# The sum of a norm's two halves moves from GpSimd to VectorE, with all queue orders written anew

## The chip, the cores and the metric

One core of one Trainium2 chip runs the whole program in a single launch. The core has five engines, each with its own queue of instructions: TensorE (PE in the profile; its weight loads are PEld), VectorE (DVE), ScalarE (ACT), GpSimd (POOL) and SyncE (SP), which here only issues DMAs. The metric is the device time in microseconds (us). Before the change the median of three runs is 1772.27 us (1771.36 to 1775.65).

## The reference

Two layers over 512 latent tokens and 256 context tokens of width 1024, in float32. Layer 0 has neighbourhood attention beside spatial gating, layer 1 has two-directional retention; each is followed by a gated MLP ("ffn") with a depthwise convolution of width 3. What the change touches is the RMS norm, which stands before and after each of these four parts:

```python
def rmsnorm(x, g):
    xf = x.astype(jnp.float32)
    y = xf * lax.rsqrt(jnp.mean(xf * xf, axis=-1, keepdims=True) + EPS)
    return (y * g.astype(jnp.float32)).astype(x.dtype)
...
        x = x + g1 * rmsnorm(y_lat, norm_g[i, 1])
        h = modulate(rmsnorm(x, norm_g[i, 2]), sh2, sc2)
        x = x + g2 * rmsnorm(conv_ffn(h, ...), norm_g[i, 3])
```

Context tokens go through layer 0 in the same way; only the 512 latent rows are returned.

## The kernel before

Tokens are cut into six tiles of 128 rows (0 to 3 latent, 4 and 5 context). A matrix product in float32 accuracy is made of three float32r products, from a high and a low part of each factor (`split`: L233 on ACT makes the high part, L234 on VectorE the low part; `mm3`: L277 to L280 on TensorE).

The program is a row of long stages (spatial gating and attention to about 330 us, ffn 0 to about 870, retention to about 1395, ffn 1 to about 1750), in which TensorE works through large products. Between two stages lies a **seam**: the output rows of one part must be normed, gated, added to the residual stream, normed again, modulated and transposed before the next part's products can begin. There are three such seams inside the program, one norm at the start (`first_x`) and one at the end, where rows only go out to memory.

For each row tile a seam runs this chain (names as in the profile):

1. L768, VectorE: `y` half = product in PSUM + partial result, two halves of 128x512.
2. L493, ACT: `Square` of each half, with its sum over the row accumulated into one column of `ss` (128x2).
3. `rms`: L498, a `tensor_scalar` on one column: first half's sum + second half's sum + eps. Then `rsq`, L479, GpSimd: that to the power -0.5.
4. L524, VectorE: `y` times the gate, half by half (needed before step 5, not before step 3).
5. L531, VectorE: residual = `y` * r + residual, half by half.
6. L493, L498, L479 again, on the residual (tiles with an x in the name: `wxc`, `xc2r`; those of step 2 and 3 have a y).
7. L543 (VectorE) and L544 (ACT) scale the two halves; then PE transposes (`ht`), and ACT and VectorE apply the modulation (L586, L588, L650, L652) and split the result.

`rms` is called 42 times: 6 at the start, 12 in the seam after attention (`wyb`, `wxb`), 12 after ffn 0 (`wyc`, `wxc`), 8 after retention (`wyd`, `wxd`), 4 at the end (`wye`). The power has no other home than GpSimd in this kernel.

The order of instructions in each engine's queue isn't the order in which the Python code makes them. `queue()` reads a compressed string, `ORDER`, that holds a permutation for each of the five queues, and chains the instructions of each engine in that order. So a waiting instruction holds up everything behind it on its engine. GpSimd's queue also holds DMA issues, among them the sums of retention's weights made by accumulating DMAs in memory (`weight_sums`, L380, tiles `tv` and `tq`), which can lie anywhere before retention uses them.

Of the kernel before, what the change touches and what calls it, by code (L numbers as in the profile page):

```python
# [56 lines left out]
g~h51h5T}T{+3ItR9jj`yQ*t0(Q17IEkLhrt!?FabCW7D0I5j4IrPdZTBoksRl?<af?MbzagN7VN?Z8M>>OpX5Q(jg^0`u~pwg99Oe4K{uDX6Fjw{z^@>
IXNLbM}~xoxEuYNQFvzM^d%(tw)p7WattQ)4wf^xNV^QA#~~_U_qB8#UE69qrA>H*8H$PucgW=!deLrD15MN^hko1t=eeN%{jdE=s|=2Kw!><5~+gI^|v
QussI+9&gZcx!HnkJHBeyY)C#6y_i1JXB!pmJytZ~5Px|@oX0T|Eq;S!iq>b4+wOvB|0(_+4q-$$-*oeV(9O4r`nlPrMrvv1f7`6#kzpbXnp&r<R@(eX9
YoE9V{04E)i?AUA!_M4(bCgRY|{`d#7K0x7uGtogo%uejx8(>duVxhga(I-gW%teR8{_n$MgxwiovU{mK`sdXrt-&I|YU@Ni(-@p+Y`1gFAJZzHyqGY^K  # L60
Y%ULKFmHa2xtWBzq<qWK=`tgNc7D_4&nsOqEcjkcO<bawK@$=<cP+B$0ai1@iU(?Z+le=g`0v`8aAfe$?<j#C5QxAPt1Ct~?g9R33SLlrkH_7A{D>imHl
=5p0@v&U1jw@@vW9Q&W*zY1!Zrn%H&^P#5%-IO|N>0cEui9^|2o)oj65q?tR;}f3{xb=zm3eq5_EuRv16ea(F{DgQz93(n;fG1qBeFx<WbnXqYOtzljP;
8krIb{@uWKwNrj;b@%M4pilu_DL$JbMaW%h38fwc4NGF6a*Nh*%ipFXyha&piknxfg%$74H#@QMBjp#rhS9;x7gLLgc?9{#C5M2Zw(VbF*`^J8*bT{H`G
1ABeZhw@Ln^ZFD1jMXbW`j?>jwCquy{+E!ILdG2Ac?|Jcn{EnEJZloO*(>HHklY^6u=e7|=Z@3Y1dZ(=J^Isg^*gZC?!c0Q9%ZFq&W<6hb5vE{~V{x#Nu
0LNi0ipwt(G5fwsdr?9cJ;z95-g&9`{~-(!XggSGi1DZ#sDNxs+vl?wIyWZ(KbFiPJ=~vAbO`bOn`Ps@d0tan1f1ZrtcJYh|{N7K#vQ5;N9X;F-Qw=?%K
MdoOiz}=<h}AYl8k&?7JfV8EAdx<oWT>qdRxkCxpA#T6|G_MCjx6d2x-9O79Td^D30~b@4U8&-21NF>VWJ`0VCYnKK66a_N>!0|Wg79}x6mL5B{rgLeiw
A`Q@)vu8Tk<L7!`5+4-<{o4U6bi-4^q35`H6MY=_IB}A0y$qr4S7a}Ia)_?Gs;lw}qK(}|YdhZ((XV_;xfm|k2O1eq+U(P@c+MHm!9Yjg=Pe<2<`|$mN7
<4$8#AInjy2UlQL6or_?Z|S`WNwI!Qh%t;@qbN)XqP~9)nnu9~YP#ZpCh1;3oKMxn?K~ydE!YU><bg?3o>eI86pCd?VSnc~yPGTe^pT(x@A#-DiV3#c^N
2Dw#!GEP|fJ(xUPxAdXG4WU>lCSKdP_t7dtMwr!=E@(PFu&8rv>Rc|%GTBYV>BH7x;5C<b_u`-@Ic3-EFvoW?JM5)Vr;<5cF%9?$r-zQp{ZLz5d57qcdH
>u7RkK0>XX8$Y3MW7-FocS&DGd6g8fOB3?qa9EHwc!wER}Xy_Up?ytF&6SHsm3tHcv5K&v862!!IPni92H&?4ZH3Y_X*k#!R#WkImk9ljyl>q+WkCfIEU  # L70
GJkLc%dx3&eXt;a1~K`a&E%+Y&A!M<H=e0*Yx?iUjiM30M)izMReGQ2MIBSBvi)crkCcSZL6K-?v(4h`HRD?ced1qktdPtbP-4E-qgv8S(>I(`Nsf)MZv
# [2281 lines left out]
```

## Time and profile before

| | |
|---|---|
| median of three runs | 1772.27 us |
| the profiled execution, own time | 1771.19 us |
| its span (first to last instruction) | 1769.4 us |
| TensorE busy | 1731.5 us (98%) |
| VectorE busy | 1434.4 us (81%) |
| ScalarE busy | 1122.4 us (63%) |
| GpSimd busy | 448.2 us (25%) |
| L498, the sum, 42 times on GpSimd | 32.09 us |
| L479, the power, in the same stretches | 25.56 us |

Busy time is the union of an engine's instructions. A number in square brackets in a timeline is the time that the engine sat idle before that instruction, and behind the arrow stands what ended the idling. A matmul's end is modelled, so a busy TensorE isn't necessarily one at its peak. A table by windows gives, for each stretch, its length, then the busy time of PE, PEld, DVE, ACT and POOL (instructions in brackets), then the granted TensorE clock, the share of time in which the DMA engines were busy, and GB/s.

### The profile page before, as it was taken

The page shows a single profiled execution, that of the slowest core. Times are in us where ns is not written, and L with a number is a line of the kernel's source. Part 1 is how long each engine was busy: PE and PEld are TensorE (multiplying, and loading weights), DVE is VectorE, ACT ScalarE, POOL GpSimd, SP SyncE. Part 2 cuts the span into 40 slices and gives each one's busy share as a digit, 9 for nine tenths or more (in the row PEclk, how much of TensorE's full clock was granted, in tenths as well). Part 3 has the DMA queues.
Part 4 walks back from the last instruction along what each step waited for, and adds up shares of the span by engine and source line. Part 5 has one row for each costly group of instructions (what it writes and reads, how often), then busy time and mean ns, then how long its engine had stood idle before and what let it go on. Part 6 is the DMA issues. An engine that isn't in the chain of part 4 may idle for free.

```text
span 1769.4 us, 29634 instructions
## 1 busy us (share of the span) xinstructions
PE 1731.5 (98%) x11108; PEld 1563.9 (88%) x11108; DVE 1434.4 (81%) x2408; ACT 1122.4 (63%) x2046; POOL 448.2 (25%) x570
## 2 busy tenths in 40 slices
...
GB/s 299 153 163 177 162 200 107 192 217 240 223 205 231 222 246 229 270 230 250 316 206 71 175 172 155 148 133 163 120 151 144 174 103 169 194 219 186 177 159 125
DMA packets 121292, 330.59 MB, mean 187 GB/s; under 512 B 14222, under 2 KB 36238, under 8 KB 120476
## 3 DMA queue, kind: packets, MB, share of 16 engines
...
## 4 chain that ended last, share of the span: by engine, by line
PE 81%; DVE 7%; ACT 4%; DMA 3%; POOL 3%; issue 2%; DVEq 0%; ACTq 0%; SPq 0%; POOLq 0%
PE px L277 10%; PE wf L278 4%; PE wf L279 4%; PE wf L280 4%; PE xv L277 4%; PE py L277 4%; PE px L280 1%; PE px L278 1%; PE px L279 1%; PE yv L277 1%; PE py L278 1%; PE py L280 1%; PE py L279 1%; PE ug L278 1%; PE wr L278 1%
## 5 line engine op out<-in xcount | busy, mean ns | idle before, releaser
L416 DVE SCALAR_TENSOR_TENSOR acc<-ar,cs,acc 128x512 f32<-128x512 f32 x256 | 188.0, 754 | 9.8 <-DMA acc<-in_adab_row 7.4
L2039 POOL DMA_DIRECT2D yf<-yp x64 | 55.7, 940 | 258.4 <-ACT yp L2035 226.6
L2035 ACT COPY yp<-wf 128x512 f32<-128x512 f32 x118 | 68.6, 584 | 70.5 <-PE wf L280 68.6
L277 PE MATMUL px<-hs,wc 128*128 128x384 f32 (+1 forms) x480 | 112.0, 309 | 0.8 <-ACT pre L1879 0.8
L277 PE MATMUL px<-blk,wb 128*128 128x384 f32 (+1 forms) x480 | 109.0, 308 | 0.0
L1892 DVE SCALAR_TENSOR_TENSOR cv<-pre,cw,cv 128x769 f32<-128x769 f32 (+1 forms) x88 | 77.6, 884 | 27.8 <-ACT cv L1891 27.5
L1891 ACT ACTIVATE cv<-pre,cw 128x770 f32<-128x770 f32 (+1 forms) x88 | 81.3, 926 | 19.3 <-DVE pre L1884 14.0
L277 PEld LDWEIGHTS px<-hs,wc 128*128 128x128 f32 x480 | 82.5, 188 | 6.7 <-ACT pre L1879 1.9
L277 PEld LDWEIGHTS px<-blk,wb 128*128 128x128 f32 x480 | 81.8, 188 | 4.7 <-ACT pre L1879 0.4
L1879 ACT ACTIVATE pre<-px 128x256 f32<-128x256 f32 (+2 forms) x160 | 54.3, 368 | 43.7 <-PE px L277 30.5
L2039 POOL DMA_DIRECT2D yd<-yp x48 | 47.4, 1020 | 124.7 <-ACT yp L2035 122.1
L1895 DVE SCALAR_TENSOR_TENSOR cv<-pre,cw,cv 128x769 f32<-128x769 f32 (+1 forms) x88 | 77.4, 884 | 1.3
L277 PE MATMUL px<-hs,wd 128*128 128x384 f32 x240 | 72.0, 338 | 0.0
L277 PE MATMUL py<-blk,wc 128*128 128x384 f32 x240 | 69.6, 337 | 0.0
L2039 POOL DMA_DIRECT2D yd<-ypg x48 | 45.7, 1006 | 86.5 <-ACT ypg L2035 73.4
L233 ACT ACTIVATE wb<-s 128x512 fp32r<-128x512 f32 x80 | 48.6, 627 | 22.1 <-PE px L277 19.1
L233 ACT ACTIVATE wc<-q 128x512 fp32r<-128x512 f32 x80 | 49.0, 629 | 17.6 <-PE px L277 6.9
L234 DVE TENSOR_TENSOR wb<-s,wb 128x512 fp32r<-128x512 f32 x80 | 54.6, 688 | 4.7 <-ACT wb L233 4.3
L234 DVE TENSOR_TENSOR wc<-q,wc 128x512 fp32r<-128x512 f32 x80 | 54.6, 688 | 4.3 <-ACT wc L233 4.0
L278 PE MATMUL wf<-fo,g 128*128 128x512 f32 x144 | 54.6, 397 | 1.2 <-ACT g L233 1.2
L280 PE MATMUL wf<-fo,g 128*128 128x512 f32 x144 | 55.5, 395 | 0.0
L279 PE MATMUL wf<-fo,g 128*128 128x512 f32 x144 | 55.2, 395 | 0.0
...
## 6 DMA issues: line engine op xcount, KB each, us to landing
...
```

The costliest lines, as they stand in the source:

```text
L233: self.S.activation(hi, src, AF.Copy)
L234: self.V.tensor_tensor(out=lo, in0=src, in1=hi.bitcast(F32), op=ALU.subtract)
L277: mm = lambda *p, **k: self.T.matmul(*p, skip_group_check=True, **k)
L278: mm(out, lhs[0], rhs[0], start=first, stop=False)
L279: mm(out, lhs[0], rhs[1], start=False, stop=False)
L280: mm(out, lhs[1], rhs[0], start=False, stop=last)
L416: V.scalar_tensor_tensor(out=acc[s], in0=raw[:, kk * 512 : kk * 512 + 512], scalar=self.cs[:, 8 * s + k : 8 * s + k + 1], in1=acc[s], op0= ...
L1891: S.activation(d, s, AF.Identity, scale=w1, bias=b)
L1892: V.scalar_tensor_tensor(out=d[:, 1:W], in0=s[:, 0 : W - 1], scalar=w0, in1=d[:, 1:W], op0=ALU.mult, op1=ALU.add)
L1895: V.scalar_tensor_tensor(out=d[:, 0 : W - 1], in0=s[:, 1:W], scalar=w2, in1=d[:, 0 : W - 1], op0=ALU.mult, op1=ALU.add)
L2035: S.copy(v, ps)
L2039: G.dma_start((yd[t] if first else y[t])[:, o], v, accum_op=ALU.add)
```

## The change

In `rms` the sum is issued to VectorE in place of GpSimd:

```diff
     def rms(self, name):
         ss = self.sst.pop(name)
         w = self.bp.tile([P, 1], F32, name=f"w{name}", tag="rsw", bufs=4)
-        self.G.tensor_scalar(out=w, in0=ss[:, 0:1], scalar1=ss[:, 1:2], scalar2=EPS, op0=ALU.add, op1=ALU.add)
+        self.V.tensor_scalar(out=w, in0=ss[:, 0:1], scalar1=ss[:, 1:2], scalar2=EPS, op0=ALU.add, op1=ALU.add)
         return self.rsq(w, name)
```

The similar sum of `rstd` (L484, six times in the spatial gating) and that of retention's own norm (L1661) stay on GpSimd. The rest of the diff replaces the whole `ORDER` string (it also grows by three lines), of which only this is readable:

```diff
 ORDER = """
-c-oD82e>3xb>_LZLRY8i?&_TTb-$c*&N<JE6W+XelXKRLq#0?XQ2?QcB!r|<0wj`z1j3jo8zF&=iN@I8{V+Dci@{)w*WNYjyx#v*zmW!P?{1G?b$4~$Tl
...
 """
```

Decoded as `queue()` does it, the two strings compare so. The instructions are the same but for the 42 sums. Those that keep their order among themselves aside, 4525 of TensorE's 10964 instructions stand elsewhere, 756 of VectorE's 2344, 547 of ScalarE's 1910, 136 of GpSimd's 524 and 104 of SyncE's 484; no instruction is moved by more than 102 places. Some places:

- **Start.** SyncE's first loads were `ar000` (weights of the modulation), `cc`, `xn04`, `xn05` (the first two row tiles); they become `xn04`, `cc`, `xn05`, `ident`, `ar000`. TensorE began with the four products of `ar000` and then had 8 transposes of rows; it now begins with a transpose, and the products of `ar000` stand between the transposes. VectorE's queue becomes sum, scaling (L515), sum, scaling, row by row.
- **After ffn 0.** VectorE's queue around the last rows (2 and 3), before and after:

```
before: L768 yf3 | L588 L588 L234 h1c  L524 yf3  L234 h1c  L524 yf3 | L531 L531 yc3r | L234 rwk
after:  L768 yf3 | L588 L524 yf3  L498 wxc2  L234 h1c  L588  L498 wyc3  L524 yf3  L234 h1c | L531 L531 yc3r | L234 rwk
```

- **After retention.** For row 0, VectorE's order becomes L768, L768, L524, sum `wyd0`, L524, L768 (row 1), L531, L531, L768 (row 1), L524 (row 1), sum `wxd0`, L524 (row 1), sum `wyd1`, L543.
- **After attention.** On GpSimd three DMA issues of the weight sums (`tq23`, `tq13`, `tv13`) move from behind the seam to between its powers of rows 0 to 2.
- **End.** VectorE's last instructions, before: L768 (row 3), L531 (row 2), L524, L524, L531, L531. After: the same, with the sum `wye3` between the second L524 and the first L531. TensorE's last 60 instructions are unchanged.

More of the change, by code (lines that the diff above doesn't have):

```diff
@@ L57 @@
[L57 to L71, printed above, removed]
@@ new lines @@
+l=*yma3U=X~e;&b@E!4$^HzlDr<mE1JQF8}9%<b^fKPHkHUp-V8oGUQ+CQUioZ_Q-sKcA3EMuwfx(gZ!)*|?Qv>;%6E<Vj?#(5bY(b{r^=1H1TF6)dP?A
+ghlPG<1>a-QmInkbS={leFlfh4C(%pdGr}y#pm)T=Nje>(CCYzNd;-@!D<X-5F9{m#dPd|bjvVImx@z{*_6a(+eDw%*muP$YB+cxcnp}4^+$BCKvR@L^Q
+gfH6qQ)kw&ynxaiq5U^56p$ap%04oc2Y034-QS<EtUqtOKHl{(e2rzD7P)uTh-ixT9D6AR4j0_rRJmrrBg(?iZp&vw0&rhMpWwT^5qL?ByA&_n#5l!O%#
+g{S5XpYWe2m_Og4ini8?8Z&f^j$DhK*$Xg|%+WMy%ND8uJWRAPUQGWo*PO++`J+d-M_=ZNMjx79bGmDM%XHG_1TPM#``Cg)G0DpS0R>dqt+$<>t@P1Pp&
+j<mQ?$fNGNcG?|vtq!|`2T$V9+DNTuHL7hrfU?Y?%w*S^PiHd~TJNb`1r>%zDtJf-J>GZ~6{(7bN6@Y!g~G&R?$oHhp`NN~V{Zf1Zqi=btZ$&*O?9<Yi+
@@ new lines @@
+4jb-W(mJhWbOTZLMv$)Zg4jyZ7wI_U68(CLV#>x=!lhDpwQ1yhx$uaI%@Al^(Ch*&2oY1p}4jiaRwnFt^LBHnAm+4Ey}PBf4>r!dz_}!C(*@so6OEqLy~
+6Vp^cv++o(XT#DB;Rv#O>`5g?<(}JEC4%C3JLD!NU8?+3oykX*a9lFKuv)?HW(gZaT!Om&K)!agj)Y43CturCC68n0(sgJseHfW!9i2CIShOTL3xE|Mx<
+M3c@9XbrV#_4=4&R4_BxDkCc>7~9&INVIX4l|fCZ#-C}AEM3lx`YK0j|TaD<`L?mcHh+PqJw5y+pe`uHMd;7jYd&}`MLSIJH-bC4V^qS{<>(mLzGtN@H>
+KUvqT3EmFRBaqr?4OokJ=&<U#SK{CoJ*--#~>Dpk?T;%-4zFN;@1k?7L&%#Xy6#rdmnw3%t#wKIBkbrdb}(?jBU@dDnnJDM7MU8QH`i-Ov&{daM$IT^k>
+)zTbUIvrX1HSwZYjlU^=F25rzlCqgU5cJn#WO!tlK7{)f>8AfFy1yX)f$#YNG4+P{Th!dFJzc)Fr<KQh&lkl{<WJ?J^3Xx_-M&q;@fW@$R?#DuF7k#4wZ
@@ new lines @@
+ZFN@eyG!_l;|I2Q1V@aIH3K;g$y|q*I1&ycQQ0KO{aZ%5S29{v(G0K%=KlK7_6N#Es&(cRW|=`n5-d+x1aFn{S(kUJxr2bcfvi34jU==T7;$nEh=WIX6o
+ml%E1(Ve8+B#-@Aa8{*b?@7cMMUqnT_zb3vfYVQ!Wb=N*Gu3e|Aiwi#%Ulm^y|12oIObuISe^l5VolSK85%HFMLcAnCDjpJ_5^Rc}5%h|fRc-TgFxMCy@
+DlxvxI&jMURua^4Gp$eQl4(RO1FzU1iw+%<xA8%vX}PsqM@-x?AU*R-v64L#|JFV{_Y+-9GMc;lr?Iz+>1o3ymuQ7^6y7b=mX*iV*oJjesQ0eq3rRgNgl
+Y<H{C7n5>E(^_fhef7^FEMM{QkIiLcvuOVHnoR&?So#r`M7KZ@3?+rA~voWdbz*XzRB>zjW?ye!mh^mXxGw^6=q63eu3w-`N5D}mm=?XVVa-Px^E_E%q^
+ZJl?BS8+$`?Msf9POnf!S74S)8#qOSb^EFI9r-v4?d_v;H&6NjAAWSkX9Rk!VEWZvY=U*Q<pTRtwAnv^zYc8d-C*3>^DjD$?TeOX-s>;C69k0e;p=n&fa
@@ new lines @@
+>t0wg4LikYhkbu-V9%k4|Gu9(ecCfVmIfV+>0{8m#<|_^zOe7saoMv6P+O6weBd23Z{aEqG=8HSuXdhK@oJILL%xYI$Ex5=km89dfzNyX6<?=C$=RXCqO
+r;@;>0{cEp4NCV#Y;a4$WbC+QeB}wyOC|ny3F;bY3y;$jTPty*X9ziVZ2bhI+1*kL>Dh*Mf<ny;5*na>xoKiGYv0^!vrK4j_y?w>@oV(DB5@KAqqne{jY
+b9K_(3<o6Tud`=rmGl-N_Q)DkXCAIMO^UtOW90~UG>6x>QoM@O~A_-B{5LSwsBhn;BIipUWRs#VI@Qc9z#A2F^2%pJSfdT=;)DaW@~a4xr&PM3cAM7bca
+aQ&b%zxg73%1%VOXCA~#(#b4v{^)m4${Lv-yS`I=ayn#;LeJ0B4bixg!?$I3CiHy3BD{~`RB=o{iK6EGeS$Bss#=(bR}y8zIDw~UUl(>yGeeu{hik@!Di
+p#OXLRUC>$AA{BAhwl{ql@xzM{6Nf1|5$tu<)prc4e$5FYXT$x>*6o4t3-PeJ}M2Qchg2=FwjD4RD)&~scGLjm6366eR^i6@wnLB_j_dz(v5w~25Ac$L|
@@ new lines @@
++jb%S*ezDA?a$6?^7WTaoQ!;<F-zSQzScR_XZ`{rsJRv<h&Yo%4>J^OZ)kKGa-A=Y|4QXd6^r#mZ=exaF~Eq^U6;qew@42PI#Wzl#W}vh9LmG*)fyqkN&
+(!6>T2DP*xmA~4}ZDi+~9lTB)Fat#D;Qr|U6v?I{D^kL!iJM8sJfxV#Fws6`{jng#H;)RL#_tHGud%jRtTLGhQX|61`wN`C$(AKtoT3@3*p=NTymMDnP@
+vN;gqcB-b_i}_fm%C|uo|2CPo9I#Th?v|lyIBNQw#TU>baA~S)H-|#fNDMeh{(XN9uTKV4~5})MvzkJCD^~3)!WB(4^`wq8B*iLt^TVWuMffLyHb%B({X
+b8;R~=jL?tGRq)*T22Ef(j-Ubu^b4Hb`dnn<pCSXM47<C4NC4g+2+B>|}vKC|@p7zspI-=+xOXP6E7dr->nlq=Shn?|sXBW*;Ql-ky<s~H^i;wJ%gT%Vj
+Fe5^+sHKBNe-PEG?E+PJSZqxB;Tmt?n?8lMPr!(5YI?2DQ9ITM?sIa(jXPeu?)A9bF~c3hfToz#lC;#XuIvC<)$HqN2OnpY%onI;sY|Z`tuDFSt4zFX0+
+)vcw0E4lnLDJhsj<?j<(c4d_lL+1j{}JJq+*mG$pU}389KAWew-Zkx6|qh{)o{wUznx3f@?5rYKkZoJG(lsk5YTtk4*<xTdKkB6pq#me91nJD>@JXphsm
@@ new lines @@
+k2Uv>5^TFW}AZged!)R4d2N)$~i6c_tmRqaceW_^V-2Gy(vN#g6Mm%7)tvSAOfyQ0niZuk>#qf5J4hz9%31%<@lx_qBQ5EA1tg3k+AGI`dLwzw=xC;a=Q
+s;}*9X~;Ics)Y>v?mr{TW@Wi0TMT-Vf}UFgqu-gO?9|~TEpoTcUuq~6J}fv5P2`SCGOY#te~T0Y}_M~CwA)`9ki-a5Bj<s1)`DE?~Bdvic}glzuQ5pyAO
+X$>^?k%UVB~aIp#?{4D)VboACL)o>#>;!0VcKkgi218@gwo6-KCez(r|h6OReCdf#g0)m5Xe)2MSLlEsCMWU&XTXn4ex*TJ(_n_X`3rf_d1AqwD?P8Ad$
+ph-ZFx;lHixN`Z5!|n;SnCt<>IT0pD9y~m2GP78GWqhZ97lmYquS&OP)kriJ-?=LiAXnY+uARH;qv3kU6L4XB0xGnS-Nu)iWDV}gJ&xY*3eh3#7!B8#$J
+tNyC@mU+CS|IksUefigQL3KZwUGgvD8P;V7MEb;uYQV-Ie!<4+<j=k4Ci5jQL1MnJza7x^7f@hiei`w_UxEh>cvmZE&c<UPYaqv}5+xTjo8UsZK_i{Crt
@@ new lines @@
+2gj|&f*pQkqFAVVB4+|>p-N-ub5!W5XbXgP!5OF#@fgq16Yi5rZ#_0p!c5O#|ETpwjTGTvVh^WD#+Pc~CZT^PAMSE+IlC}zTSh}Bb`Jfrm`!j7Zw<{DjD
+AO@f!>S8CTG{HRa79N+2Tt}<ot`4k5Y^_GfVkZ08%hpgIustR8(tr-WY)JF01N5fct#A+fR~I|ycIx9iqC)i!y=&8ww+mLR6Bm+_%3c{b2~n_rwkn-%<%
+bnB$Az7N+2;_VjBptY_U61+~eTZAus}}2!|lSOr3Oa3WKj$4G-D$Net2I$~>h{_9eS1oMw4ePX%%}#(QZyZ5#KG`gYaFVFn2Io)KSSKlN1|yqja!wRF@G
+2TfR^A<dUg1uKh2yok}QsfMwz@}%K#oKXfnU8+h?H$a5zAU}x);0;FT6XIS`YIEHsrly+5Xt=UF80bUfE_Bwo-C*|ji~3wUbumrxRJ6H=M-pC-uO&qbZE
+EfEQiod4|ALcK5e42plW{cHfEaM|Sgl6CBsR0^MbHO|*S4vqQe8Wnrw$iG{?TJc_kb$-3O;;>71&SpE{eHoT2s{LibkqcYKzk_hOgANZJg5<&J<0IFuNK
@@ new lines @@
+!4h$LcD6ldY^TK#_U$39)dO<7OJE~z(p1RtxQJ1@^pUn%mN~Lvr3qop^HUSN(pmS~Ao;x>R)(DyE84O)KmM?&aqz#`97CZ0zD0rn04&Gi_%-V|CGxJqY&
+BXw<p9a=XcLh;0`_kx`Zo~*y;dUV$R`f;u#6AR$T2~wEUX7Vz+^U=#ucI?(`v+k2?tGZ*#A+-xy1cZk8^vz#SfrZ8`Fe@%4F$8pL=RSjBNS>E^I4O5pO}
+k8t8_kGQ_XrD&^<IbRIF4}6zIsn@t+4_`lL8l-@rjNQdb+lUv$rzFu?uoI^Erj@Ch%A#rsws6BjRa_m;e-adL*~YDFNc6$tj(PK%MwvUc`RS0_yOUeWbU
+leE1ks&2a}5rTwgjEVw=Pf_c81lh!0#-A}Wh`_#{6i<oT;~x~jsLzO}#kCWR5<{{45L_>GANm;XT6A^5lkz?LPt9#yJZ0!`2~ef{!~v~T#WsvR@Z5^537
+hqBHtMg@b6oM>8b5rSs&jCdR3Mnm_^4y9DNA{qucf&q0dor^j`eHs#%N?7X1tb5CZ_`+627XoiS5k+4icH3Ika&x)O~YrUoSYaGZU_@<11+w#zbkWX9B~
@@ new lines @@
+*3;_}y-+Scb7+3ekYXAYd<Tx~3-eS$-cDesX{80QvJS2h3_sQ>yx5eGEg1#@*?~3HbOMfYxhiH@jjj%r@UlbeAO;evT3G_>XwqdJ~U)!htH}PM^Z;Lm@*
+Tqg+|EBo4cn12WSowYN=Yk0y9e+wZDNapa;S3Vg<#yUf2ll7U+{tbr;wA#+U?RCTun8#|i;s;)Os!1+Tl@o$OQU%faT)ZqXg*9ImLHNQj-Plz9OV&x245
+$h6GuNT;FNcW=S+_LxMZOmr4z@|Id_`*2X<ljfsYRmv7qHQeNeCq(AE~I51FbQ+x7>yPT@2bf-2j{qk^6gkC$0E=ShfIag=kK{KoFjn@s<U;&lOr|0O|R
+7G~)B6OsE3@fA_dR{R*he#3kdeM$Vf_#g5ez7!lS{RX!&&7Ad1fPmM~kIx9=HZgQCC1Q`TJCbHL(qyX*oVI#Kd`(dJ9s$~ArU#iVkeT&(P>fDIxTU<!Zs
+6R(j9fsQ8@G+MUA)xJ2GVnWKH#mPi$jD@xHFw$QQ4^s)Yh?~QMhK1MjAaM!=Rtz+r~{jJ#dh-5@0$-u1GqC!A&L_5A3IPHPL#5-?3wMjvw7)fVvFA<%a3
@@ new lines @@
+D6&UBvrmD%QN<P}%xr!KjW|cCI?&YO6NAD_Nw6(2uD9rR3qCC=?Sfpmy1-KXu0<Mc!E>lf10VAKHiH426rbw*X1eEQ_m#)}u-x{OUd?Ru1wH?65MvuNwx
+trx0C-dmY;ZoJ7IrWl1b&~nWjlQ{E9FggiRoT0-_fN%2#g#wC&I<gz%rRnhrG(M?FOY5JH|5Kt2(C-J_C71$6nh=^=j5Z3*1s<3WAbUqc1TajC*@0G@bH
+nFPTxevD}vZm=+YZJ5?>e3$W1!@1u=2h`JDWWe5tI?nQh*9eVi?NVPg9-5pLAK-QG`AcAEc}S|2q1%-O9AnMO|;prAWuZ{&E;>als)?zow~HgjeCaZlMS
+*y72)tkB#JvQ8>9-96sjdv@<YAa8}gbWwK?s1cI~cHIe@nx^vY2Zw0XEP!tW-wOtAR40uc>uVh*3Ne#wQ8_&dMA}q$GV{ip)iaB}6h(SC88tZMQ*A*q6?
+Ukif%fg<+Og6!b9P<a4h7@W(PL9@g7?<3)Hr^{Ro~6kKXsB$*HZt3tmE$!L%VjuDeBM@$BqtF(cz(sUB`|Bq{lCtsl69O+cN^2bo!>oJ46=4a{4Cp$87m
@@ new lines @@
+l{QiaffuIjzh%bWHFg&dPg*cL>-;$q}bR9zdD#&b#apW2K4f&RQPQEB@&&k|@yTm8tOP0If`-h*Fw~LPpavUQd0IK>Ly!qm#C*@P}RdF1s0et_2u+vNO8
+L3?&I)CBICJq5GMt~eQ@1tjN<k_-05GQU4O7GL+{e!;Z<^J!1ii1#v+QZ+>^c~_|zdQ48Dy?h>OPt~1!J6kdM+kb@{WQcQO`F-%vaOIAy>HxOW_r7_ura
+;es!Zt1!>WCGiN*Q)T6m0)E-WsD`_OZ+huL@=?#MeYO;GJ6x&@=Yoi1J)Z6+MBtFt^ku(tv6f~N)m6$hZkdWa);&%VulRL-)|aFV4Nlr?<v@R4?nEyMu-
+z+Kfib?4v$wJe}Hyzks)pWU^SI8(Mvb*~A!02AzPJ&Q1T@)RBC*`&Sbi{tkSl9A|W?}^&FqsM?12M-Ov3Z4*6`wr5`FxciPoc_3|tGzV&Fd`OBR6i}~WH
+~jy_{SU^IL8GNw{O#N^goL~69>!*i8sZ8JH!UP1ru2NfnWfCQ_x=l6{zwD;#=~!BozH)lCJgB-288fhb6?f#Ha!oXk+hl7}>9iy^KMd`*<Sb03H9Vd>h5
```

200 lines of the change are left out of this document (81 added, 119 removed).

## The prediction

> **What bounds the kernel now.** I read the page's head first, then a table of the five places where norms run, one window for each, and in the same windows the sums alone.
>
> ```profile
> span 1769.4 us, 29634 instructions
> PE 1731.5 (98%) x11108; PEld 1563.9 (88%) x11108; DVE 1434.4 (81%) x2408; ACT 1122.4 (63%) x2046; POOL 448.2 (25%) x570
> ...
> 0.00:30.00 30.00, 20.81 (x93) 9.72 (x94) 6.54 (x16) 18.16 (x46) 8.11 (x21) 0.89 0.79 283
> 330.00:390.00 60.00, 58.91 (x320) 51.04 (x317) 53.50 (x90) 44.07 (x101) 22.05 (x31) 1.00 0.68 213
> 870.00:912.00 42.00, 37.70 (x214) 31.58 (x213) 37.92 (x62) 31.28 (x75) 20.85 (x28) 1.00 0.93 291
> 1394.00:1428.00 34.00, 29.51 (x172) 25.25 (x172) 30.60 (x56) 24.76 (x60) 11.11 (x16) 0.95 0.50 175
> 1745.00:1770.00 25.00, 16.47 (x72) 13.10 (x70) 16.13 (x25) 6.05 (x17) 7.15 (x9) 0.92 0.33 105
> sum 191.00, PE 163.39 PEld 130.69 DVE 144.69 ACT 124.32 POOL 69.27; mean PE 32.68 PEld 26.14 DVE 28.94 ACT 24.86 POOL 13.85
> ```
>
> TensorE is the bound: it idles 1769.4 - 1731.5 = 37.9 us in all. The windows hold 191.0 - 163.4 = 27.6 us of it: 9.2 at the start, 1.1 after attention, 4.3 after ffn 0, 4.5 after retention, 8.5 at the end. The long stages hold the other 10.3. The change doesn't touch the work of TensorE, so these gaps are all that it can shrink, and within the seams VectorE, at 53.5 of 60 and 37.9 of 42 us, is nearly as full as TensorE.
>
> The next table has the same windows for L498 alone; the last fence is the sum line of the same table for L479.
>
> ```profile
> 0.00:30.00 30.00, 3.42 (x6) 0.89 0.79 283
> 330.00:390.00 60.00, 9.06 (x12) 1.00 0.68 213
> 870.00:912.00 42.00, 10.39 (x12) 1.00 0.93 291
> 1394.00:1428.00 34.00, 6.08 (x8) 0.95 0.50 175
> 1745.00:1770.00 25.00, 3.13 (x4) 0.92 0.33 105
> sum 191.00, POOL 32.09; mean POOL 6.42
> ```
>
> ```profile
> sum 191.00, POOL 25.56; mean POOL 5.11
> ```
>
> A sum of one column takes 32.09 / 42 = 0.76 us on the average. Why so long shows in the timelines of VectorE and of GpSimd at the last rows after ffn 0, with TensorE's largest wait there:
>
> ```profile
> 899.82 0.98 DVE L588 TENSOR_SCALAR hc<-htc,ab 128x256 f32<-128x256 f32 x2
> 900.72 0.68 DVE L234 TENSOR_TENSOR h1c<-hc,h0c 128x512 fp32r<-128x512 f32 x1
> 901.32 0.68 DVE L524 TENSOR_TENSOR yf<-yf,fin 128x512 f32<-128x512 f32 x1
> 901.92 0.68 DVE L234 TENSOR_TENSOR h1c<-hc,h0c 128x512 fp32r<-128x512 f32 x1
> 902.53 0.68 DVE L524 TENSOR_TENSOR yf<-yf,fin 128x512 f32<-128x512 f32 x1
> 904.55 1.41 DVE L531 SCALAR_TENSOR_TENSOR fin<-yf,yc3r,fin 128x512 f32<-128x512 f32 x2 [1.35 <-POOL yc3r L479]
> ```
>
> ```profile
> 900.21 0.30 POOL L498 TENSOR_SCALAR wxc<-ssxc 128x1 f32<-128x1 f32 x1 [2.96 <-ACT jxc L493]
> 900.82 2.54 POOL L498 TENSOR_SCALAR wyc<-ssyc 128x1 f32<-128x1 f32 x1 [0.31 <-DVE hc L588]
> 903.45 0.56 POOL L479 TENSOR_TENSOR xc2r<-wxc,mhalf 128x1 f32<-128x1 f32 x1
> 903.97 0.55 POOL L479 TENSOR_TENSOR yc3r<-wyc,mhalf 128x1 f32<-128x1 f32 x1
> ```
>
> ```profile
> PE rkc L280 <- DVE rwk L234: 2.0, 1, 2.0
> ```
>
> The first sum takes 0.30 us while VectorE reads PSUM (L588). The second takes 2.54: it ends at 903.36, when VectorE has run dry after four operations with both inputs in SBUF. Only then do two powers follow, VectorE waits 1.35 us, and TensorE 2.0 us for what is queued behind. So a sum on GpSimd is held while VectorE streams, and then holds VectorE. The Trainium skill says it as a rule (SBUF — State Buffer, Who interferes with whom): a VectorE instruction with two SBUF inputs contends with a GpSimd one that reads SBUF, and the second to start waits for the whole of the first. The trace agrees, with 2.54 us against 0.30.
>
> **The change part by part. The sum on VectorE.** No row shows it there. Nearest are two operations on one or two columns (ns: min, median, max):
>
> ```profile
> L1213 DVE RECIPROCAL sst<-sst x32: 138/156/165, 188.7 to 326.5; 128x1 f32<-128x1 f32 x32
> L1167 DVE TENSOR_SCALAR sst<-sst x8: 148/187/753, 202.6 to 326.6; 128x2 f32<-128x2 f32 x8
> ```
>
> I take 0.16 us, by the row with one column; the other end is 0.75, the longest of the row with the same operation. VectorE thus gets 42 x 0.16 = 6.7 us more work, of which 32 x 0.16 = 5.1 lie in the three inner seams. It cannot be a gain below nothing: VectorE did none of it. Each sum is queued in order: behind it wait the gate products, residuals and splits that feed TensorE.
>
> **The power** stays on GpSimd, at 0.56 us where nothing holds it, and it too reads SBUF. I take it that it is held only where the new order has two-input operations right behind the sum.
>
> **After ffn 0.** In the new order, from 899.82: L588 (0.49), L524 (0.60 from start to start), sum (0.16), L234 (0.60), L588 (0.49), sum `wyc3` (0.16), so its result is there at 902.3; then L524 and L234 to 903.5. If the power gets in at once, it ends at 902.3 + 0.08 (hand-over, as between 903.36 and 903.45) + 0.56 = 902.96, and L531 starts at 903.5, 1.05 earlier than 904.55. If it is held until VectorE is dry, it ends at 903.5 + 0.56 = 904.1, 0.45 earlier. I take -0.7, which comes off the 2.0 that TensorE waits.
>
> **After retention.** VectorE's longest waits for powers there are these:
>
> ```profile
> DVE xd L531 <- POOL yd3r L479: 0.8, 1, 0.8
> DVE yr L543 <- POOL xd0r L479: 0.7, 1, 0.7
> ```
>
> If both vanish, 1.5 us go; eight sums add 8 x 0.16 = 1.3. In the first row the second L524 and row 1's L768 now stand between sum and residual, so little of the time won is used. Between -1.5 and +1.3 I take -0.4.
>
> **After attention** TensorE idles 1.1 us at most. Twelve sums add 1.9 us to VectorE, and three DMA issues stand between the powers; I take -0.2, with -1.1 and +1.9 as ends.
>
> **The end.** The last rows on VectorE, then on GpSimd:
>
> ```profile
> 1761.51 0.69 DVE L768 TENSOR_TENSOR yf<-wf1C,yf 128x512 f32<-128x512 f32 x1 [0.18 <-PE wf1C L280]
> ...
> 1762.77 1.28 DVE L524 TENSOR_TENSOR yf<-yf,G 128x512 f32<-128x512 f32 x2
> 1764.82 1.41 DVE L531 SCALAR_TENSOR_TENSOR fin<-yf,ye3r,fin 128x512 f32<-128x512 f32 x2 [0.76 <-POOL ye3r L479]
> ```
>
> ```profile
> 1763.11 1.03 POOL L498 TENSOR_SCALAR wye<-ssye 128x1 f32<-128x1 f32 x1 [2.83 <-ACT jye L493]
> 1764.22 0.56 POOL L479 TENSOR_TENSOR ye3r<-wye,mhalf 128x1 f32<-128x1 f32 x1
> ```
>
> Here 1.03 us of GpSimd's sum stand on the path, and one would book them as won. But the new order puts `wye3` behind both L524, which end at 1764.05. Then 0.16 + 0.08 + 0.56 + 0.04 give 1764.9 for L531, against 1764.82: +0.1, nothing won.
>
> **The start.** SyncE's first issues and TensorE's first work:
>
> ```profile
> 0.72 0.39 SPq L219 DMA_DIRECT2D ar<-in_adaw  x1
> ...
> 1.63 0.91 SPq L219 DMA_DIRECT2D xn<-in_x  x2
> ```
>
> ```profile
> 4.95 3.42 PE L328 MATMUL ad<-ar,cs 128*2 128x256 f32 x8 [4.95 <-ACT cs L285]
> 11.16 0.44 PE L2136 MATMUL ht<-ident,xn 128*128 128x128 f32 x2 [2.79 <-DVE xn L515]
> 13.00 1.33 PE L2136 MATMUL ht<-ident,xn 128*128 128x128 f32 x5 [1.40 <-DVE xn L515]
> ```
>
> Loading `xn04` first puts it 0.9 us earlier by its place in the queue alone, more if it no longer shares the bandwidth with `ar000`; the transposes at 11.16 and 13.00, which end 2.79 + 1.40 us of idling, come earlier by as much. Against it, the four products that filled TensorE from 4.95 now come later and need room. The sum itself wins little: the second row's now stands behind the first row's scaling. Between 0 and -2 I take -1.0.
>
> **The long stages** are reordered too, with 10.3 us of idling in them. I can't read a sign from permutations this fine, and take 0, with -5 and +5 as ends.
>
> The sum: -0.7 - 0.4 - 0.2 + 0.1 - 1.0 = -2.2. The profiled execution took 1771.19 us (its span and 1.8 around it), 1.1 below the median of the runs; so 1769.0 for one like it and **1770.1** for the median. 0.3% of it, 5.3 us, is about what a measurement of this kernel can tell from no change.
>
> **The rivals. The power inherits the wait.** If the lock is the cause, taking one of two short reads off GpSimd leaves the other to be held as long. For it: the sum always comes first of the pair and takes the blow, and the powers after it found VectorE dry. Then 32.09 - 42 x 0.30 = 19.5 us of holding pass to L479, and the chain saves a sum of 0.30 and pays one of 0.16. Only the start's -1.0 is left, and VectorE's 5.1 us in the seams fill what it idled: about 1772. Such is the skill's rule (same section) taken to its end; a sentence of its page Perfetto Trace Analysis (Optimizing Scalar/DVE Operations), that moving work between the two "might not help" as they share a port, goes the same way. Chance 0.20.
>
> **The new order closes gaps everywhere.** Of 37.9 us, the end's 8.5 and the first 4.95 can't go; 24.5 can. A third of that is 8: 1764. For it, more than a third of TensorE's instructions stand elsewhere; against it, the largest gaps are in seams that I have costed. Chance 0.22.
>
> **Slower: sums hold up VectorE.** A sum waits in order for ACT's second `Square`, which ends some time after L531 or L768, and the splits behind it wait too. VectorE idles 6.5 + 4.1 + 3.4 = 14.0 us in the inner seams; 32 sums at 0.16 leave 8.9, so it decides from 0.28 us of waiting for each sum. At 0.5 each, 32 x 0.66 = 21 us less 14 are +7: 1779. Against it, the orders shown put one or more operations ahead of most sums. Chance 0.12.
>
> **How the numbers follow.** The forecast keeps 0.46. Below 1767.0 (faster by over 0.3%) lie 0.20 of the second rival and 0.04 of the forecast: 0.24. Above 1777.6 lie 0.10 of the third. The rest, 0.66, is no change that can be told. The range, 1764.5 to 1775.5, leaves out the third rival and half of the second's lower part.
>
> **What would show it.** No L498 on GpSimd, 42 on VectorE at 0.16 (0.75 would make the third rival). L479's 25.56 us about as before, or near 45 by the first rival. The wait of 1.35 for `yc3r` at 0.5 or less, and TensorE's idle time after ffn 0 near 3.6. From the last L768 to the last L531 3.3 us as now; if that is 2.5, my reading of the end is wrong. The first transpose at 10 us or earlier. I'm wrong if TensorE's idling in the long stages moves by more than 5 us.

## The result, and the profile after

The changed kernel takes 1763.3 us in the median of four runs, the kernel before 1772.9 in the same measurement: a ratio of 0.9943, with a 95% interval of 0.9923 to 0.9962. That is 9.5 us off, where I had forecast 2.2 off and a range down to 1764.5. A measurement beside later runs gave 0.9945 (0.9927 to 0.9962). One of the four runs, the profiled one, was disturbed (3036 us at a clock of 0.72), so the ratio leaves it out and the profile below is of a later run of the same program. Its lines stand three further down: the sum is L501, the power L482, the residual L534, the product with `wf1` L771, the gate product L527.

The head of its page:

```profile
span 1761.5 us, 29638 instructions
PE 1729.0 (98%) x11108; PEld 1562.6 (89%) x11108; DVE 1438.5 (82%) x2450; ACT 1124.6 (64%) x2047; POOL 416.7 (24%) x528
```

To see where the 7.9 us of the span went, I cut both traces at places up to which the two orders have issued the same set of products. The time between two cuts then holds the same work of TensorE in both. The rows are, before and then after: the start, feed-forward 0, the seam after it, the middle of retention, retention's last part, feed-forward 1, and the end.

```profile
0.00:16.53 16.53, 7.39 (x23) 3.08 (x24) 3.33 (x5) 7.86 (x21) 5.97 (x16) 0.85 0.86 310
430.00:896.40 466.40, 462.87 (x2401) 420.42 (x2401) 406.94 (x588) 279.00 (x493) 154.49 (x189) 1.00 0.98 240
896.40:918.12 21.72, 18.88 (x151) 17.90 (x150) 19.54 (x33) 17.78 (x36) 5.63 (x8) 1.00 0.85 273
918.12:1274.65 356.53, 351.21 (x2632) 332.72 (x2632) 250.67 (x409) 220.37 (x346) 72.33 (x86) 1.00 0.53 142
1274.65:1369.12 94.47, 94.27 (x736) 91.06 (x735) 63.80 (x114) 63.99 (x101) 22.92 (x26) 1.00 0.58 147
1457.85:1761.47 303.62, 303.62 (x2101) 280.14 (x2099) 272.28 (x425) 207.97 (x375) 62.52 (x74) 1.00 0.69 175
1761.47:1769.40 7.93, 0.00 (x0) 0.00 (x0) 3.96 (x6) 0.72 (x2) 1.59 (x2) 0.78 0.54 207
```

```profile
0.00:15.23 15.23, 7.04 (x23) 3.14 (x24) 4.02 (x8) 9.75 (x23) 3.45 (x12) 1.00 0.86 314
428.70:893.50 464.80, 462.89 (x2401) 420.48 (x2401) 410.29 (x601) 279.33 (x494) 147.61 (x179) 1.00 0.98 243
893.50:914.16 20.66, 18.77 (x150) 17.79 (x150) 20.66 (x38) 18.93 (x39) 3.71 (x5) 1.00 0.58 193
914.16:1263.90 349.74, 347.81 (x2632) 331.83 (x2632) 247.75 (x408) 222.78 (x347) 73.07 (x89) 1.00 0.56 147
1263.90:1359.46 95.56, 94.50 (x735) 91.01 (x735) 65.73 (x109) 62.02 (x100) 19.70 (x24) 1.00 0.52 131
1448.22:1752.80 304.58, 304.58 (x2101) 280.68 (x2099) 272.69 (x428) 209.49 (x376) 60.02 (x71) 1.00 0.69 174
1752.80:1761.50 8.70, 0.00 (x0) 0.00 (x0) 4.75 (x8) 0.72 (x2) 0.59 (x2) 0.63 0.54 206
```

The two stretches between these rows (the first large products with the seam after attention, and the seam after retention with what follows it) kept their lengths to 0.03 us.

Read two things. First, retention's middle, to which I gave nothing, shrank by 356.5 - 349.7 = 6.8 us. Feed-forward 0 gave 1.6, the start 1.3 and the seam after feed-forward 0 gave 1.1. Retention's last part took 1.1 more, feed-forward 1 another 1.0 without any idle time, and the end 0.8 more. So the long stages gave 6.3 us net and the places that I had costed 1.6. (Feed-forward 0's 1.6 is not shown to be the change's: in a second profile of the kernel before, the same products took 468.6 us, 2.2 more than in the first.) Second, TensorE's idle time fell from 37.9 to 1761.5 - 1729.0 = 32.5 us, 5.4 less. The remaining 2.5 came out of its *busy* time, 1731.5 to 1729.0, for the same 11108 matmuls. The prediction had said that the gaps are all that can shrink.

None of the 42 moved sums lies in retention's middle, so I began there. TensorE's waits in it, before and then after:

```profile
PE xv L277 <- ACT rg L1466: 1.3, 3, 0.6
PE rt L1684 <- DVE rg L1671: 1.1, 2, 0.6
PE ro L278 <- ACT of L1633: 0.9, 4, 0.3
PE rs L278 <- ACT rq L233: 0.7, 1, 0.7
PE ro L278 <- ACT sd L233: 0.4, 1, 0.4
PE xk L277 <- ACT ks L1405: 0.2, 1, 0.2
PE ro L280 <- DVE sd L234: 0.2, 1, 0.2
```

```profile
PE rs L281 <- ACT rq L236: 1.2, 1, 1.2
PE ro L281 <- ACT sd L236: 0.4, 1, 0.4
PE zv L281 <- ACT rwv L236: 0.3, 1, 0.3
```

Thirteen short waits for ScalarE and VectorE became three. With those too short for this list (under 0.15 us each), TensorE stalled 18 times before and 4 times after. The three lines that are gone first (`rg`, `rt`, `of`) were 9 waits of 3.3 us.

### The profile page after: what moved, and what is told of

Its sections match the earlier page's. It is cut to its first block, busy times and chain, and to the rows that moved or that the text cites. A ratio compares the mean times of both kernels' runs of the same rounds, so it can differ in the third digit from the quotient of the medians.

```text
span 3034.6 us, 29638 instructions
## 1 busy us (share of the span) xinstructions
PE 3015.1 (99%) x11108; PEld 2381.7 (78%) x11108; DVE 1458.3 (48%) x2450; ACT 1138.9 (38%) x2047; POOL 412.5 (14%) x528
## 4 chain that ended last, share of the span: by engine, by line
PE 99%; issue 0%; DVE 0%; DMA 0%; SPq 0%; POOL 0%; DVEq 0%; POOLq 0%; ACT 0%
PE px L280 12%; PE wf L281 5%; PE wf L282 5%; PE wf L283 5%; PE py L280 4%; PE xv L280 4%; PE px L282 2%; PE px L281 2%; PE px L283 2%; PE yv L280 2%; PE py L283 2%; PE xk L280 2%; PE py L282 2%; PE py L281 2%; PE ug L281 1%; PE ug L283 1%
## 5 line engine op out<-in xcount | busy, mean ns | idle before, releaser
L280 PE MATMUL px<-hs,wc 128*128 128x384 f32 (+1 forms) x480 | 174.6, 447 | 0.0
L280 PE MATMUL px<-blk,wb 128*128 128x384 f32 (+1 forms) x480 | 173.2, 450 | 0.1
L280 PEld LDWEIGHTS px<-blk,wb 128*128 128x128 f32 x480 | 113.7, 250 | 29.2 <-issue 12.7
L280 PEld LDWEIGHTS px<-hs,wc 128*128 128x128 f32 x480 | 113.1, 247 | 28.4 <-issue 13.5
L280 PE MATMUL px<-hs,wd 128*128 128x384 f32 x240 | 111.9, 512 | 0.0
L280 PE MATMUL py<-blk,wc 128*128 128x384 f32 x240 | 109.9, 514 | 0.0
L283 PE MATMUL wf<-fo,g 128*128 128x512 f32 x144 | 81.4, 571 | 0.0
L281 PE MATMUL wf<-fo,g 128*128 128x512 f32 x144 | 81.0, 575 | 0.0
L282 PE MATMUL wf<-fo,g 128*128 128x512 f32 x144 | 80.7, 575 | 0.0
L280 PEld LDWEIGHTS px<-hs,wd 128*128 128x128 f32 x240 | 59.6, 249 | 25.0 <-issue 14.2
L280 PEld LDWEIGHTS py<-blk,wc 128*128 128x128 f32 x240 | 60.6, 253 | 21.4 <-issue 9.1
L237 DVE TENSOR_TENSOR wb<-s,wb 128x512 fp32r<-128x512 f32 x80 | 54.3, 687 | 46.3 <-ACT wb L236 45.8
L280 PE MATMUL px<-hs 128*128 128x256 f32 x240 | 76.3, 385 | 0.0
```

The costliest lines, as they stand in the source:

```text
L237: self.V.tensor_tensor(out=lo, in0=src, in1=hi.bitcast(F32), op=ALU.subtract)
L280: mm = lambda *p, **k: self.T.matmul(*p, skip_group_check=True, **k)
L281: mm(out, lhs[0], rhs[0], start=first, stop=False)
L282: mm(out, lhs[0], rhs[1], start=False, stop=False)
L283: mm(out, lhs[1], rhs[0], start=False, stop=last)
```

## The experiments

Two theories at first: the gain is the newly searched order's (theory 1), or it is that of the moved sum (theory 2). The first kernels split the change in two; the next put the old or the new relative order of all queues into one stretch only; the last try what adds up, and the end. In the kernels of mixed order, an instruction changes its place only among those that start in the stretch. The intervals are of the ratio to the kernel before.

**The change once more, its code alone, its order alone.** The first has no edit. The second keeps before's queue orders, with each sum put on VectorE where GpSimd began it; the third has after's orders and this:

```diff
-        self.V.tensor_scalar(out=w, in0=ss[:, 0:1], ...
+        self.G.tensor_scalar(out=w, in0=ss[:, 0:1], ...
```

> The changed kernel once more, for a profile to set beside the one of before. Both theories expect some 1763 us, 9.5 below before. They differ in where TensorE's 37.9 us of idling shrink. Theory 1 (the newly searched order closes small gaps everywhere): the start's 9.2 us fall by 1 to 3 and the long stages' 10.3 by 4 or more, the seams by 1 to 3. Theory 2 (taking the held sum off GpSimd frees VectorE and so TensorE): the three inner seams' 9.9 us fall by 5 or more, and the long stages stay within 2 us. Theory 3 (the power inherits the wait, and hides a larger gain): L479, now L482, rises from 25.56 us to near 45.

> The sums on VectorE, all else in the queue orders of before: each sum stands before the first VectorE operation that started after GpSimd had started that sum in the trace of before. Theory 1 (the order): 1770 to 1776 us, no gain, since the places of the sums were not searched. Theory 2 (the sum's engine): 1763 to 1767 us. If sums wait in VectorE's queue and hold it up (the rival on the slow side): 1777 or more.

> The new queue orders with the 42 sums put back on GpSimd, each right before its power. Theory 1 (the order): 1762 to 1767 us, most of the 9.5 us kept. Theory 2 (the sum's engine): 1770 us or more, since the order was searched for a sum that costs VectorE's time and GpSimd is held as before.

| | median us | ratio | interval |
|---|---|---|---|
| the change | 1763.1 | 0.9945 | 0.9927 to 0.9962 |
| the code alone | 1769.9 | 0.9984 | 0.9971 to 0.9998 |
| the order alone | 1762.2 | 0.9939 | 0.9918 to 0.9959 |

With its sums back on GpSimd, the new order keeps the whole gain. So theory 2 falls: with these orders the edit that gives the change its name is worth nothing that can be measured. With the old orders it is worth about 2 us. In the first run the idle time moved as theory 1 expected: that of the start and that of the seam after feed-forward 0 fell by 0.95 us each, and that of the four long stretches above by 4.2. But the length of those four fell by 6.3.

**The new order in retention's middle alone, and all but there.** The first is the kernel before with the new relative order between 918.1 and 1274.8 us: 1197 of 2631 matmuls, 143 of 408 instructions of VectorE, 110 of 334 of ScalarE, 20 of GpSimd and 15 of SyncE change their place. The second is the changed kernel with the old relative order there. One of the places in TensorE's queue, in head 2:

```diff
   ro20  L279
-  yv
   ro20  L280
-  yv x4
+  yv x8
   ro21  L278
```

> The kernel before, with its sums on GpSimd, and the new relative order of all five queues only for what starts between 918.1 and 1274.8 us of the trace of before (retention's middle). No sum of a norm lies there. In the changed kernel this stretch took 349.7 us instead of 356.5. Theory A (the gain is the stretch's own: fewer stalls of TensorE): 6.8 us off, 1764 to 1767 us, 4 or 5 stalls of TensorE in the stretch instead of 18. Theory B (the stretch gains because of what comes before it or beside it, the start, the seams or the sums): less than 2 us off, 1770 us or more.

> The changed kernel with its sums on VectorE, and the old relative order only for what starts between 914.1 and 1263.9 us of its trace (the same stretch). Theory A (the gain is the stretch's own): 6 to 7 us back, 1768 to 1770 us, some 18 stalls again. Theory B: 1763 to 1765 us.

Measured: 1766.6 us (0.9971, 0.9958 to 0.9984) and 1772.0 us (0.9996, 0.9983 to 1.0009). The stretch in the one, then in the other:

```profile
919.81:1269.44 349.63, 347.91 (x2632) 331.84 (x2632) 246.31 (x409) 220.92 (x345) 70.42 (x86) 1.00 0.53 144
```

```profile
916.53:1272.45 355.92, 351.26 (x2632) 332.86 (x2632) 249.30 (x406) 218.97 (x344) 73.67 (x88) 1.00 0.53 143
```

With the new order 349.6 us and 4 stalls, with the old one 355.9 and 17, whatever stands around it: theory A holds for the stretch. The medians moved by 4.8 and 8.9 us, not by 6.8 and 6.8: the rest of the change shows nothing in the time with the old order in retention, and some 4 us with the new one (ratios of 0.9971 without it and 0.9945 with it). In both profiles the seam ahead ran at a granted clock of 0.92 to 0.93 and took 1.4 us longer (see the last section); in the second one the part behind the stretch idled 0.8 us more as well. Neither was tried by itself, and why the two steps differ so much stays open.

How an order takes stalls away shows at the place of the diff. TensorE and then ScalarE in the kernel before:

```profile
1080.79 0.29 PE L280 MATMUL ro<-rv,sd 128*128 128x256 f32 x1
1080.91 0.28 PE L277 MATMUL yv<-rwg,s41r 128*128 128x256 f32 x1
1081.03 0.40 PE L277 MATMUL yv<-rwg,s40r 128*128 128x256 f32 x2
1081.26 0.28 PE L277 MATMUL yv<-rwg,s41r 128*128 128x256 f32 x1
1081.75 0.38 PE L278 MATMUL ro<-rv,sd 128*128 128x256 f32 x1 [0.21 <-ACT of L1633]
1081.97 0.29 PE L279 MATMUL ro<-rv,sd 128*128 128x256 f32 x1
```

```profile
1081.11 0.58 ACT L1633 COPY of<-ro 128x512 f32<-128x512 f32 x1
```

and with the new order in the stretch:

```profile
1079.92 0.28 PE L277 MATMUL ro<-rv,sd 128*128 128x256 f32 x1
1080.04 0.28 PE L274 MATMUL yv<-rwg,s40r 128*128 128x256 f32 x1
...
1080.85 0.28 PE L274 MATMUL yv<-rwg,s41r 128*128 128x256 f32 x1
1080.96 0.30 PE L275 MATMUL ro<-rv,sd 128*128 128x256 f32 x1
```

```profile
1080.24 0.58 ACT L1630 COPY of<-ro 128x512 f32<-128x512 f32 x1
```

ScalarE's copy empties the tile `ro` of one chunk before the next chunk's first product may start. From that chunk's last product to the release it takes 1081.75 - 1080.79 = 0.96 us; products start every 0.117 us, so it is 8.2 steps long, and seven or eight products are needed in between. The old order had four, the new one has eight. Seven of the 18 stalls are of this kind, four at `ro` and three at `xv` (which the copy to `rg` empties): 0.95 to 1.07 us from the last product to the next, with one to five products in between. In the kernel with the new order in the stretch one such place is left, with five in between and 0.10 us idle; in neither kernel does a place with six or more show any idling. The other eleven stalls waited for other results of ScalarE and VectorE; how the order removed most of those was not followed.

The same rows give the price of a stall. From 1081.26 to 1081.97 there are two steps, 0.23 us if nothing stalls; they took 0.71, so 0.48 are lost. The profile shows 0.21 of it as idle. The rest hides in the records of matmuls: the last one before the stall is booked 0.28 although its successor could have started after 0.12, and the one after it takes 0.22 to its successor. Over the stretch, with 14 stalls fewer, the length fell by 6.90 and the idle time by 5.32 - 1.72 = 3.60: 3.30 / 14 = 0.24 us net for each stall beyond what is shown as idle. Taken stall by stall, against the usual step of 0.118 us between the starts of two products, the hidden part is 0.24 to 0.46 us, 5.4 us for the 18. So the 14 stalls took 7.9 us with them, and short delays elsewhere in the stretch gave 1.0 back. The Trainium skill (TensorE: Matmul & The Clock Gate, Single matmul latency) says of a bf16 matmul that it pays a nearly fixed drain through the array beside its columns, about 175 ns. The record's 0.28 - 0.12 = 0.16 us is close to that; but the ends of the records are modelled, so it is no measurement of the drain.

**The start alone, and the kernel before once more.** The first has the new relative order before 33 us only; the second has no edit.

```diff
 SyncE's loads
+  xn04
   ar000
...
-  xn04
```

> The kernel before, with the new relative order only for what starts before 33 us, sums on GpSimd. If the new order of the first loads pays as I booked it: the 17th matmul ends 1 us or more earlier than the 16.5 us of before, and TensorE's idle time up to there falls from 9.1 to about 8. If the 1.3 to 1.8 us that the three other runs show there are the transfers' own scatter: no steady difference from the repeat of before that is run beside it.

> The kernel before once more, for a second profile, to see what differs between two executions of one program. If its order decides: 18 stalls in retention's middle and 356 to 357 us for it, as in the first profile, and TensorE idle 9 us up to the 17th matmul. If the start's idle time is scatter of the transfers: it comes out 1 us or more away from 9.1.

The first 17 products ended at 14.8 us, with 8.2 us of idling ahead of them. In three profiles with the old order and the sums on GpSimd they ended at 16.5, 16.1 and 16.7, with 9.1, 8.4 and 8.9. So the new order of the start is worth 1.3 to 1.9 us there, beyond the scatter of 0.6. (It moves 11 of SyncE's instructions and 35 of the other engines'; the loads by themselves were not tried.) The moved sum in the old order of the start ended them at 14.9 in the code alone, but at 16.0 in the kernel of the next experiment, so its worth there is not shown. Up to one and the same product, near 30 us, the three old profiles took 29.1 to 29.9 us, the two with the moved sum 28.4 and 29.1, and the eight with the new order of the start 26.7 to 27.6. In the repeat of before, retention's middle took 356.55 us with 18 stalls, against 356.53 and 18: that loss is no scatter. Single times, 1772.5 and 1773.8, can't tell 1.5 us.

**The sums and retention's order together.** The code-alone kernel, with the new order in retention's middle only; the diff is that of the two kernels above.

> The sums on VectorE in the old queue orders (as in the kernel with the code alone), and the new relative order only in retention's middle, 916.0 to 1271.2 us of that kernel's trace. The code alone gave 1769.9 us, retention's order alone took 4.8 us off 1771.5 in the medians and 5.5 to 6.9 off that stretch. Theory A (two causes that add up: retention's order, and the sums in the seams and the start): 1762 to 1765 us, so that the new order everywhere else is worth nothing. Theory B (the rest of the new order is needed too): 1767 us or more.

It took 1762.8 us (0.9948, 0.9932 to 0.9965), all of the change's gain. So the time is theory A's: retention's order and the moved sum give all of it. Retention's order and the new order of start and seams gave it too (the order alone, above). So by the medians these two are substitutes, not terms that add. Up to feed-forward 0 the traces agree: the product that started between 429.8 and 431.0 us in the three profiles with neither came at 428.1 and 428.2 with the moved sum in the old orders, and at 426.6 to 428.5 in the eight with the new order of the start.

**The end.** In the changed kernel I moved the last sum in VectorE's queue, and then the last but one too. Beside the second ran the unedited change.

```diff
+  L501 wye2
   L771 yf13
-  L501 wye2
   L527 yf12
...
+  L501 wye3
   L527 yf13 x2
-  L501 wye3
   L534 fin x2
```

> The changed kernel with its last sum, wye3, one place in front of the two last gate products on VectorE instead of behind them. From the start of the last product with wf1 (L771) to the start of the last residual (L534) the changed kernel took 3.33 us. If the place of the sum was what ate the gain at the end, as I argued: 2.6 to 3.0 us, if the power gets in beside the gate products at once or after one of them. If the power is held until VectorE has run dry (the power inherits the wait): 3.2 us or more, and L482 for ye3r takes over 1 us.

> The changed kernel with the last two sums moved on VectorE: wye3 in front of the two last gate products, and wye2 in front of the product with wf1 (L771) that it stood behind. In the changed kernel VectorE waited 0.44 us for ye2r and 0.66 for ye3r, and TensorE's last product ended 8.73 us before the end; with wye3 alone moved it was 8.38. If both waits are the places of the sums: neither wait is left, the end takes 7.7 to 7.9 us, and the time is 0.8 to 1.0 below that of the changed kernel beside it. If wye2's power is held beside L771 as beside the gate product: 8.2 to 8.4 us and 0.4 below.

> The changed kernel beside the one with the two moved sums, on the same chip: 1763.1 us, the end 8.6 to 8.8 us; 0.4 to 1.0 us above its neighbour, by how much the places of the last two sums decide.

VectorE in the unedited change, then with both sums moved (its lines stand three less: L501 is L498 there), and its GpSimd:

```profile
1751.28 0.21 DVE L501 TENSOR_SCALAR wye<-ssye 128x1 f32<-128x1 f32 x1
1751.40 0.68 DVE L527 TENSOR_TENSOR yf<-yf,G 128x512 f32<-128x512 f32 x1
1752.52 0.75 DVE L534 SCALAR_TENSOR_TENSOR fin<-yf,ye2r,fin 128x512 f32<-128x512 f32 x1 [0.44 <-POOL ye2r L482]
...
1756.51 1.42 DVE L534 SCALAR_TENSOR_TENSOR fin<-yf,ye3r,fin 128x512 f32<-128x512 f32 x2 [0.66 <-POOL ye3r L482]
```

```profile
1752.55 0.21 DVE L498 TENSOR_SCALAR wye<-ssye 128x1 f32<-128x1 f32 x1 [0.19 <-ACT jye L493]
1752.68 1.28 DVE L524 TENSOR_TENSOR yf<-yf,G 128x512 f32<-128x512 f32 x2
1753.88 1.41 DVE L531 SCALAR_TENSOR_TENSOR fin<-yf,ye3r,fin 128x512 f32<-128x512 f32 x2
```

```profile
1749.32 0.54 POOL L479 TENSOR_TENSOR ye2r<-wye,mhalf 128x1 f32<-128x1 f32 x1 [2.85 <-DVE wye L498]
1752.84 0.92 POOL L479 TENSOR_TENSOR ye3r<-wye,mhalf 128x1 f32<-128x1 f32 x1 [2.99 <-DVE wye L498]
```

From TensorE's last product to the end it takes 8.78 us unedited, 8.38 with `wye3` moved and 7.85 with both; neither wait is left. With `wye3` alone moved, L771 to L534 took 2.86 us instead of 3.33 (one time, 1760.7 us). The medians are 1761.5 against 1763.0 beside it, in the expected direction, though the runs overlap (1760.1 to 1765.0 and 1761.3 to 1763.8). It has the lowest median of all versions timed more than once; its ratio (0.9940, 0.9927 to 0.9953) can't be told from that of the change or of the order alone. The power tells why the place matters: 0.54 us beside L768, which reads PSUM, and 0.92 beside the gate product, which reads SBUF twice.

**Old order where the new one was longer.** The changed kernel with the old relative order in retention's last part and from 1448.3 us on.

```diff
 every queue, 1263.9 to 1359.4 us and from 1448.3 us on
-  the new relative order
+  that of the code-alone kernel
```

> The changed kernel, with the relative order of the code-alone kernel in the two stretches where the new one took longer: retention's last part (95.6 us against 94.5 of before) and the last feed-forward with the end (304.6 and 8.7 against 303.6 and 7.8). If these three differences are the order's own: 3 us off, 1759 to 1761 us. If they are scatter: 1762 to 1764 us.

It took 1762.8 us: nothing won in the time. The busy time of feed-forward 1 did fall back, from 304.6 to 304.8 - 1.0 = 303.8 us, and the end to 7.8; but one new stall of 1.0 us appeared at the edge. Retention's last part stayed at 95.1 us, so its 1.1 did not come back. So only feed-forward 1's and the end's, 0.8 and 0.9 us, are seen to be the order's own, and mixing two orders gave half of them back.

## Why the prediction was wrong

**The bound.** TensorE as the bound was right. "These gaps are all that it can shrink" was not: a third of what went (2.5 of 7.9 us) was booked as busy. The Trainium skill warns of it (Perfetto Trace Analysis, Identifying the Most-Contended Engine): the busy share of matmuls doesn't say how close TensorE is to its limit. I had quoted the idle time and taken it as a ceiling.

**The long stages are the step that failed**: "I can't read a sign from permutations this fine, and take 0, with -5 and +5 as ends." They gave 6.3 us net, and retention's middle alone 6.8. Both halves of the step failed. The ends leaned on the 10.3 us of idling, and the 18 stalls in retention's middle cost 5.3 us of idling and 5.4 more. And a sign could be read: at a stall like that of `ro21`, one counts the products between the last one into a tile and the next that needs it. The sign of being wrong that I had named, idling in the long stages that moves by more than 5 us, would have missed it too: in the four stretches it moved by 4.2.

**The rivals.** The second (the new order closes gaps everywhere, 1764, chance 0.22) gave the time. Its mechanism was half right: the new order, but mostly one stage and not everywhere. What I held against it, that the largest gaps are in seams that I had costed, weighed single gaps and not their number. The first rival shows in full only where the old order stands: there `yc3r`'s power took 2.07 us and VectorE still waited 0.44 for it. In all, L479's 48 powers went from 29.95 us to 34.71 with the code alone and to 31.85 with the new orders, not to near 50. One reading of mine was too simple there: by the rule that I quoted, what is held waits for one VectorE operation, and that is what powers of 0.86 to 0.93 us show; but the sum of 2.54 us and the power of 2.07 waited for a whole run of them. The third (sums hold up VectorE) did not come: with the sums on VectorE in the old orders the time fell to 1769.9 us, and in the new orders it is the same wherever the sums are.

**The sum** at 0.16 us: its record says 0.20 to 0.21, but the next instruction starts 0.12 to 0.13 after it, so 42 cost about 5.3 us of VectorE's queue. Right in size.

**After ffn 0**, -0.7: VectorE's wait of 1.35 for `yc3r` is gone and the seam took 20.7 us for 21.7, so -1.0. The moved sum by itself does what I had forecast: in the old order it took the seam to 21.0 us, in both kernels that have it so.

```profile
894.07:915.10 21.03, 19.10 (x149) 17.89 (x148) 19.91 (x36) 17.53 (x36) 3.58 (x4) 1.00 0.89 279
```

But the new order does it without the sum: with the sum on GpSimd (held for up to 1.45 us), TensorE idled 1.7 us in that seam, with the sum on VectorE 1.9, where it idled 2.8 before. VectorE and GpSimd in the changed kernel:

```profile
899.27 0.20 DVE L501 TENSOR_SCALAR wyc<-ssyc 128x1 f32<-128x1 f32 x1
...
900.66 1.41 DVE L534 SCALAR_TENSOR_TENSOR fin<-yf,yc3r,fin 128x512 f32<-128x512 f32 x2
```

```profile
899.62 0.86 POOL L482 TENSOR_TENSOR yc3r<-wyc,mhalf 128x1 f32<-128x1 f32 x1 [0.31 <-DVE wyc L501]
```

The power is held for 0.3 us and is done before VectorE comes to L534.

**After retention**, -0.4: 0.0 measured, though VectorE's waits for powers there fell from 2.0 us to 0.4; TensorE's wait for `hb` grew from 1.7 to 2.5 in their place. **After attention**, -0.2: +1.0 measured, before and then after:

```profile
330.01:374.76 44.75, 43.98 (x232) 36.48 (x229) 39.18 (x65) 33.16 (x81) 19.51 (x27) 1.00 0.66 196
```

```profile
327.19:372.94 45.75, 44.36 (x233) 36.08 (x229) 41.00 (x78) 33.58 (x82) 11.99 (x16) 1.00 0.68 189
```

That is the order's, and not the twelve sums': with the sums moved in the old orders the same products took 44.8 us, with the new orders and the sums on GpSimd 45.8. **The end**, +0.1: L771 to L534 took 3.33 us, as forecast. But I had looked at `wye3` only. `wye2` now stands behind L771 and ahead of a gate product, its power took 0.92, and L771 started 0.7 us later after TensorE's last product: +0.8. **The start**, -1.0: -1.3 measured for the first 17 products, -2.3 up to 30 us. The first transpose came at 7.7 us, 3.4 earlier and not 0.9; what `xn04` won there, the four products that came later took back, as the forecast said in kind.
